# A two-layer hybrid decoder on one core: delta-rule heads in a fixed TensorE order, block diagonals filled by DMAs, S5's loads issued earlier

## The chip, the core and the metric

The kernel runs on one core of a Trainium2 chip. The core has five engines with queues of their own: PE (TensorE: matrix products), DVE (VectorE), ACT (ScalarE), POOL (GpSimd) and SP, which here only issues DMAs; POOL and ACT issue some as well. Each engine takes its queue in order, and engines wait for one another and for DMAs by semaphores. The metric is the device time of one execution, in microseconds (us).

## What is computed

x is (1024, 1024), in float32, and there are two layers. Both have the same frame: one input projection, a mixer beside a 4-head cross-attention into 256 memory tokens, one output projection over their concatenated outputs, a layer norm, an MLP with squared ReLU (1024 to 4096 to 1024) and a second layer norm.

```
def step(state, inp):                       # layer 0, per head (8 heads of 128), chunk after chunk
    v_new = ui - wi @ state                 # ui, wi: from a triangular solve inside the chunk
    attn = (qi @ ki.T) * deci
    o = (qi * exp(gci)) @ state + attn @ v_new
    state = state * exp(g_last) + (ki * exp(g_last - gci)).T @ v_new
...
st = sr + abar^t * h                        # layer 1: S5, diagonal complex scan, 64 groups of 16 channels
y  = Re(C st) + d_skip * u;  zg = gelu(y);  out = zg * sigmoid(zg @ w_glu + b_glu)
...
h = concatenate([mix, cross]) @ w_o[i]
x = layer_norm(alpha * x + h);  x = layer_norm(alpha * x + relu(x @ w1)**2 @ w2)
```

In layer 0, queries, keys and values go through a causal convolution of width 4 and SiLU, queries and keys are normalised, and the output of each head is normalised and multiplied by SiLU of a fourth projection, the gate. The triangular solve uses the inverse of (I + strictly lower part of beta k k^T times the decay) of each chunk.

## The kernel before

All big products are float32 in three fp32r products (`mm3`, L120 to L125): the weight and the activation are both split into a high and a low part. A projection of 128 columns (`proj_fm`) is 2 halves of 512 tokens times 8 steps of 128 inputs times 3, 48 products of 128x512. Its weight comes by an SP DMA into one of two raw buffers, and is split by ACT (L102) and DVE (L103) into one of two pairs of buffers.

The program is written as a sequence, and a scheduler gives each engine an order by readiness and program order. `piece()` (L73) fixes TensorE's order for what stands in it: its products go behind all those of the piece before.

Layer 0 works in tiles of 128 tokens, 8 per head, in two halves of 4:
- `gdn_a(h)` (L469) makes the keys of head h: projection, convolution, norm; the decay matrix D from prefix sums (`decay`, L457); the products `kk` (L501) and the strictly lower matrix NT, written to DRAM: its 32x32 diagonal blocks, packed by POOL into `pkd` (L508), and two masked copies (L512, L513).
- `gdn_inverse(h0)` (L516) inverts the 32x32 diagonal blocks of two heads at once, with a block in each partition: 8x8 blocks by scalar products on DVE, a round trip through DRAM (L565 to L577), then 16x16 products on POOL (L582 to L587), and the result into DRAM (L597, L598).
- `block_diag` (L600) loads such blocks packed and spreads them over a block-diagonal 128x128 tile with a DVE multiplication by a mask (L605).
- `gdn_invert_tiles` (L609) goes from 32 to 64 to 128 with five groups of four products `iv` (L623) per half, each needing the one before through DVE (`zi`, L628) or ACT.
- `gdn_b(h)` (L642) makes queries, values and gate, the inversion, and the recurrence over the 8 tiles (L698 to L726): `ks` = K S; `R` on DVE (L710); `pe` = T R (L712); `e` on ACT (L714); the outputs `po` (L716, L717); `pS` (L720); `S` on DVE (L725). Norm, transposes (`ot`, L740) and gate follow, and a DMA to `cat`.

The run takes keys three heads ahead: keys 0 and 1, the inverse of heads 0 and 1, the cross-attention with keys 2 in it, and then for each head `gdn_b(h)`, keys h+3 and, after an odd head, `gdn_inverse(h+1)`, which needs the keys of heads h+1 and h+2. In the program the inversion of a head comes behind its own queries, values and gate.

In layer 1, `s5_front` (L1293) orders pieces: U (S5's projection), Q, S, T, V (the attention's), `drive` and `read`. `s5_drive` (L1137) loads, for eight groups in two halves, G (`g1d`), two tables and H (`h1d`) by POOL DMAs, makes p1 = G u on TensorE (L1166), rotates by the tables on DVE and ACT, scans on DVE (L1175), rotates back, and lastly issues the load of the matrix M0 (`zd`). `s5_read` (L1188) makes y from M0 u and H r.

Of the kernel before, what the change touches and what calls it, by code (L numbers as in the profile page):

```python
# [28 lines left out]
class Trunk:  # L29
# [125 lines left out]
    def acc_tm(self, tau, hk, wk, add, banks=("pi", "po", "sc")):  # L155

        t0 = (tau % 4) * P
        n = len(wk)
        for c in range(2):
            ps = self.psum(banks[self.turn % 3], "tm")  # L160
            self.turn += 1
            for k in range(n):
                hi, lo = hk[k][tau // 4]
                self.mm3(ps, (hi[:, t0:t0 + P], lo[:, t0:t0 + P]), wk[k][c], k == 0, k == n - 1)
            add(c, ps)

# [102 lines left out]
    def gdn_consts(self):  # L269
# [25 lines left out]
        bd = scr[:, 3 * P:3 * P + 4]  # L295
        nc.gpsimd.memset(bd, 0.0)
        for b in range(4):
            nc.gpsimd.memset(bd[32 * b:32 * b + 32, b:b + 1], 1.0)
        self.bdm = bd
        self.early = [early[:, 2 * P + 64 * n:2 * P + 64 * (n + 1)].rearrange("p (t h) -> p t h", t=8) for n in range(2)]  # L300
        cw = scr[:, 3 * P + 8 + 13 * 64:].rearrange("p (m j) -> p m j", j=4)
# [54 lines left out]
    def gates(self, ba):  # L356
# [37 lines left out]
        gc, wd, egl, nec = self.gc, self.wd, self.egl, self.nec = G("gc"), G("wd"), G("egl"), G("nec")  # L394
# [16 lines left out]
        V.tensor_scalar(nec, nec, -1.0, None, op0=ALU.mult)  # L411
        self.beta = beta

        self.ssk, self.gam, self.ngam, self.kds, self.sk = G("ssk"), G("gam"), G("ngam"), G("kds"), G("sk")
# [16 lines left out]
    def conv_silu(self, m, xT, outs, tag, w=None):  # L431
# [17 lines left out]
        self.proj_fm(w or self.a["w_in"][m], xT, evac, "wi")  # L449
# [7 lines left out]
    def decay(self, h, hf, tag):  # L457

        nc = self.nc
        pb = self.sums(h, hf, tag)  # L460
        d = self.tile(tag, [P, 4, P], F32, "D")
        for t in range(4):
            tt = 4 * hf + t
            nc.vector.scalar_tensor_tensor(d[:, t, :], pb[:, t, :], self.gc[:, tt, h:h + 1], self.maskneg, op0=ALU.subtract, op1=ALU.min)
        nc.scalar.activation(d, d, AF.Exp)
        nc.scalar.dma_start(self.ded[h, hf], d)
        return d

    def gdn_a(self, h, xT, w=None):  # L469

        nc = self.nc
        V = nc.vector
        kT = self.kTs[h % 4]
        self.conv_silu(8 + h, xT, [kT[:, :HALF], kT[:, HALF:]], "h1", w)
        for hf in range(2):
            t4 = slice(4 * hf, 4 * hf + 4)
            pt = self.psum("pa", "kt", (P, 4, P))
            for t in range(4):
                tt = 4 * hf + t
                nc.tensor.transpose(pt[:, t, :], kT[:, tt * P:(tt + 1) * P], self.ident)  # L480
            for t in range(4):
                tt = 4 * hf + t
                nc.scalar.activation(self.jk, pt[:, t, :], AF.Square, accum_out=self.ssk[:, tt, h:h + 1])
            s = lambda x: x[:, t4, h]
            V.tensor_scalar(s(self.ssk), s(self.ssk), 4e-6, None, op0=ALU.add)
            V.reciprocal(s(self.gam), s(self.ssk))
            V.tensor_tensor(s(self.gam), s(self.gam), s(self.beta), op=ALU.mult)
            V.tensor_scalar(s(self.ngam), s(self.gam), -1.0, None, op0=ALU.mult)
            V.tensor_tensor(s(self.kds), s(self.gam), s(self.wd), op=ALU.mult)
            nc.gpsimd.tensor_tensor(s(self.sk), s(self.ssk), self.half[:, 0:4], op=ALU.pow)  # L490
            kd = self.tile("h1", [P, 4, P], F32, "kd")
            for t in range(4):
                nc.scalar.activation(kd[:, t, :], pt[:, t, :], AF.Copy, scale=self.kds[:, 4 * hf + t, h:h + 1])
            nc.sync.dma_start(self.kdd[h, hf], kd)
            d = self.decay(h, hf, "h1")
            pq = self.psum("pa", "kk", (P, 4, P))
            n = self.tile("h1", [P, 4, P], F32, "NT")
            for t in range(4):
                tt = 4 * hf + t
                c = slice(tt * P, (tt + 1) * P)  # L500
                nc.tensor.matmul(pq[:, t, :], kT[:, c], kT[:, c], start=True, stop=True)  # L501
            for t in range(4):
                tt = 4 * hf + t
                V.scalar_tensor_tensor(n[:, t, :], pq[:, t, :], self.ngam[:, tt, h:h + 1], d[:, t, :], op0=ALU.mult, op1=ALU.mult)
            pkd = self.tile("S", [P, 4, 32], F32, "pkd")
            for b in range(4):
                q = slice(32 * b, 32 * b + 32)
                nc.gpsimd.tensor_copy(pkd[q], n[q, :, q])  # L508
            nc.gpsimd.dma_start(self.ntd[h, t4].rearrange("t b j i -> (b j) t i"), pkd)
            for w, m in enumerate((self.m64, self.m128)):  # L510
                nm = self.tile("h1", [P, 4, P], F32, "nm")
                nc.gpsimd.tensor_tensor(nm, n, m.unsqueeze(1).to_broadcast([P, 4, P]), op=ALU.mult)  # L512
                nc.gpsimd.dma_start(self.ntf[h, hf, w], nm)  # L513
        return kT
# [85 lines left out]
    def block_diag(self, h, hf, w):  # L600
        nc = self.nc
        pk = self.tile("S", [P, 4, 32], F32, "pk")
        nc.sync.dma_start(pk, self.t32[w, h, 4 * hf:4 * hf + 4].rearrange("t b i c -> (b i) t c"))
        o = self.tile("h4", [P, 4, 4, 32], F32, "bd")
        nc.vector.tensor_tensor(o, pk.unsqueeze(2).to_broadcast([P, 4, 4, 32]),  # L605
                                self.bdm.unsqueeze(1).unsqueeze(3).to_broadcast([P, 4, 4, 32]), op=ALU.mult)
        return o.rearrange("p t b c -> p t (b c)")

    def gdn_invert_tiles(self, h, hf):  # L609
# [3 lines left out]
        T32, V32 = self.block_diag(h, hf, 0), self.block_diag(h, hf, 1)  # L613

        def masked(w):
            o = self.tile("h4", [P, 4, P], F32, "nm")
            nc.sync.dma_start(o, self.ntf[h, hf, w])
            return o
# [17 lines left out]
        zi = plus_i(mm4(masked(0), T32))  # L636
        T64 = keep(mm4(V32, zi), "h4")
        V64 = keep(mm4(zi, V32), "h4")
        zi2 = plus_i(mm4(masked(1), T64))
        return keep(mm4(zi2, V64), "h3")  # L640

    def gdn_b(self, h, xT, kT):  # L642
        nc = self.nc
        V = nc.vector

        qT = [self.tile("h2", [P, HALF], F32, "qT") for _ in range(2)]
        self.conv_silu(h, xT, qT, "h2")
        qe = []
        at, vs = (x.rearrange("p (t c) -> p t c", t=8) for x in self.mix[2 * (h % 2):2 * (h % 2) + 2])
        for hf in range(2):  # L650
            pt = self.psum("pa", "qt", (P, 4, P))
            for t in range(4):
                nc.tensor.transpose(pt[:, t, :], qT[hf][:, t * P:(t + 1) * P], self.ident)
            for t in range(4):
                nc.scalar.activation(self.jk, pt[:, t, :], AF.Square, accum_out=self.ssq[:, 4 * hf + t, h:h + 1])
            d = self.tile("h2", [P, 4, P], F32, "Dq")
            nc.sync.dma_start(d, self.ded[h, hf])
            pb = self.sums(h, hf, "h2")
            e = pb.rearrange("p t i -> p (t i)")
            nc.scalar.activation(e, e, AF.Exp)  # L660
            V.tensor_tensor(e, e, qT[hf], op=ALU.mult)
            qe.append(e)
            pq = self.psum("pa", "qk", (P, 4, P))
            for t in range(4):
                tt = 4 * hf + t
                nc.tensor.matmul(pq[:, t, :], kT[:, tt * P:(tt + 1) * P], qT[hf][:, t * P:(t + 1) * P], start=True, stop=True)
            for t in range(4):
                tt = 4 * hf + t
                V.scalar_tensor_tensor(at[:, tt, :], pq[:, t, :], self.gam[:, tt, h:h + 1], d[:, t, :], op0=ALU.mult, op1=ALU.mult)
        V.tensor_scalar(self.ssq[:, :, h], self.ssq[:, :, h], 5.12e-4, 5.12e-4 * 4e-6, op0=ALU.mult, op1=ALU.add)  # L670

        vT = [self.tile("h2", [P, HALF], F32, "vT") for _ in range(2)]
        self.conv_silu(16 + h, xT, vT, "h2")
        for hf in range(2):
            pt = self.psum("pa", "vt", (P, 4, P))
            for t in range(4):
                nc.tensor.transpose(pt[:, t, :], vT[hf][:, t * P:(t + 1) * P], self.ident)
# [874 lines left out]
```

## Time and profile before

| | us |
|---|---|
| median of three runs (lowest, highest) | 2930.1 (2928.14, 2931.73) |
| the profiled execution | 2924.6 |
| its span in the profile | 2922.9 |
| busy: PE, DVE, ACT, POOL | 2769.2, 1752.8, 994.0, 536.4 |
| first recurrence product of heads 0 and 5 at | 227.4, 660.5 |
| first transpose after the output projection of layer 0 at | 896.2 |

The page cuts the span into 40 slices of 73 us: layer 0's heads fill slices 0 to 11, its MLP follows, S5's front lies around 1725 to 2000, and the rest is the output projection and MLP of layer 1. A row of the order of time reads: start, length, engine, line, operation, output from inputs, shape, count, and in brackets how long the engine stood idle before it and what ended that. In a group's row the busy time comes first, the mean length in ns, then idle time.

### The profile page before, as it was taken

What the parts mean: (1) busy time and instruction counts of PE and PEld (TensorE: products, weight loads), DVE (VectorE), ACT (ScalarE), POOL (GpSimd) and SP (SyncE); (2) the same over time, 40 slices, a digit from 0 to 9 for tenths busy, and PEclk for the clock granted to TensorE, in tenths of its full rate; (3) what the DMA queues carried; (4) which work ended last, traced back from release to release, by engine and by line L of the source; (5) the groups of instructions that cost most, each with busy time, mean ns of one, the idle gap of its engine ahead of it and who ended that gap; (6) DMA issues with size and microseconds to landing.
All of it is one profiled execution on the core that took longest, in us unless ns stands there. A gap on an engine that the chain in (4) does not pass through costs nothing. (4 is left out here: it accounts for less than half of the span.)

```text
span 2922.9 us, 35948 instructions
## 1 busy us (share of the span) xinstructions
PE 2769.2 (95%) x13373; PEld 2261.3 (77%) x13373; DVE 1752.8 (60%) x3467; ACT 994.0 (34%) x2104; POOL 536.4 (18%) x785
## 2 busy tenths in 40 slices
PE   8999898888999999999999988879999999999998
PEld 6877676666788888778788877768888888888887
DVE  7766667665678687665655654464587444434446
ACT  5455344443422332232322234353222222222221
POOL 3631625535002021211110111212001000000002
PEclk9999999999999999999999999989999999999999
DMA  5433334333531132222222165555331111111111
GB/s 190 109 111 97 90 104 117 101 106 76 191 94 53 64 116 81 91 76 71 76 74 82 69 205 151 165 146 184 119 101 65 51 51 48 46 51 51 44 51 58
DMA packets 177583, 279.72 MB, mean 96 GB/s; under 512 B 86608, under 2 KB 103200, under 8 KB 177408
## 3 DMA queue, kind: packets, MB, share of 16 engines
q1 hardware_dynamic: 155776, 220.29, 23.9%
q0 software_dynamic: 19328, 52.94, 6.1%
q10 hardware_dynamic: 2304, 4.20, 0.4%
q8 instruction: 105, 1.72, 0.2%
q14 instruction: 70, 0.57, 0.1%
HBM read 209.73 MB, written 67.60 MB: 95 GB/s over the span
## 5 line engine op out<-in xcount | busy, mean ns | idle before, releaser
L260 DVE TENSOR_TENSOR y<-tm,y 128x512 f32<-128x512 f32 x448 | 308.5, 690 | 204.4 <-PE tm L125 200.5
L123 PE MATMUL w<-xTh,w1h 128*128 128x512 f32 x1024 | 400.6, 391 | 0.1
L124 PE MATMUL w<-xTl,w1h 128*128 128x512 f32 x1024 | 399.4, 390 | 0.0
L125 PE MATMUL w<-xTh,w1l 128*128 128x512 f32 x1024 | 399.0, 390 | 0.0
L123 PE MATMUL tm<-w2h,hh 128*128 128x512 f32 x1024 | 398.9, 390 | 0.0
L125 PE MATMUL tm<-w2h,hl 128*128 128x512 f32 x1024 | 398.6, 389 | 0.0
L124 PE MATMUL tm<-w2l,hh 128*128 128x512 f32 x1024 | 398.5, 389 | 0.0
L115 ACT CAST w2h<-w2r 128x512 fp32r<-128x512 f32 x128 | 76.4, 622 | 554.7 <-PE tm L125 445.8
L184 POOL TENSOR_SCALAR mv<-mv 128x1 f32<-128x1 f32 x32 | 40.5, 1266 | 1166.4 <-DVE mv L183 1166.4
L125 PEld LDWEIGHTS w<-xTh,w1l 128*128 128x128 f32 x1024 | 192.2, 188 | 40.4
L125 PEld LDWEIGHTS tm<-w2h,hl 128*128 128x128 f32 x1024 | 192.2, 188 | 39.9
L124 PEld LDWEIGHTS tm<-w2l,hh 128*128 128x128 f32 x1024 | 192.2, 188 | 39.9
L123 PEld LDWEIGHTS w<-xTh,w1h 128*128 128x128 f32 x1024 | 192.1, 188 | 39.9 <-ACT xTh L199 0.8
L123 PEld LDWEIGHTS tm<-w2h,hh 128*128 128x128 f32 x1024 | 192.2, 188 | 39.7
L124 PEld LDWEIGHTS w<-xTl,w1h 128*128 128x128 f32 x1024 | 192.3, 188 | 39.5
L213 DVE TENSOR_TENSOR hl<-w,hh 128x512 fp32r<-128x512 f32 x128 | 87.3, 688 | 167.8 <-ACT hh L212 167.8
L103 DVE TENSOR_TENSOR w1l<-w1r,w1h 128x1024 fp32r<-128x1024 f32 x62 | 75.9, 1225 | 186.1 <-ACT w1h L102 184.1
L123 PE MATMUL wi<-xTh,wih 128*128 128x512 f32 x384 | 159.1, 414 | 3.5 <-ACT zc L687 3.5
L125 PE MATMUL wi<-xTh,wil 128*128 128x512 f32 x384 | 157.6, 410 | 0.0
L124 PE MATMUL wi<-xTl,wih 128*128 128x512 f32 x384 | 157.5, 410 | 0.0
L208 ACT ACTIVATE w<-w 128x512 f32<-128x512 f32 x128 | 74.5, 582 | 167.0 <-PE w L125 161.2
L102 ACT CAST w1h<-w1r 128x1024 fp32r<-128x1024 f32 x62 | 65.4, 1054 | 185.5 <-PE w L124 154.6
(417 smaller groups left out, 5711.3 us busy)
## 6 DMA issues: line engine op xcount, KB each, us to landing
w1r<-in_w_dram SPq DMA_DIRECT2D x64, 512.0 KB, 3.4
w2r<-in_w_dram SPq DMA_DIRECT2D x64, 512.0 KB, 3.4
wir<-in_w_in_dram SPq DMA_DIRECT2D x24, 512.0 KB, 3.6
wor<-in_w_o_dram SPq DMA_DIRECT2D x24, 512.0 KB, 3.5
cat<-cat SPq DMA_DIRECT2D x24, 512.0 KB, 3.3
gb<-gcd SPq DMA_DIRECT2D x32, 256.0 KB, 4.2
ntf<-nm POOLq DMA_DIRECT2D x32, 256.0 KB, 2.9
nm<-ntf SPq DMA_DIRECT2D x32, 256.0 KB, 3.3
```

Of the source, the lines that this page charges most:

```text
L102: nc.scalar.copy(hi, r)
L103: nc.vector.tensor_tensor(lo, r, f32(hi), op=ALU.subtract)
L115: nc.scalar.copy(hi, s)
L123: nc.tensor.matmul(ps, a[0], b[0], start=start, stop=False)
L124: nc.tensor.matmul(ps, a[0], b[1], start=False, stop=False)
L125: nc.tensor.matmul(ps, a[1], b[0], start=False, stop=stop)
L184: nc.gpsimd.tensor_scalar(mv[:, 2:3], mv[:, 1:2], 1e-5, None, op0=ALU.add)
L208: nc.scalar.activation(ps, ps, AF.Relu)
L213: nc.vector.tensor_tensor(lo, ps, f32(hi), op=ALU.subtract)
L260: nc.vector.tensor_tensor(o, ps, o, op=ALU.add)
```

## The change

- `proj_steps`, `acc_steps` and `gdn_recur` are generators that yield after each small step with its length on TensorE in us. `weave` runs one step of a main generator, then steps of a fill worth `share` us, each in a piece of its own, so that TensorE's order is that of the program. `take` runs steps up to a sum.
- `gdn_recur(h)` is the main part. The fill is `gdn_fill(h+1)`: keys of head h+3, queries, values and gate of head h+1 (`gdn_projections`), with the ten inversion steps of head h+1 spread among them. The first of these steps is due 2.3 us into the fill (half of 49 / 10.5). `gdn_inverse(h+1)` is called in the projections of the odd head h, behind its queries and the keys of head h+2, so while the recurrence of head h-1 runs. The last recurrence is woven with the output projection.
- `gdn_a` becomes `gdn_keys` and `gdn_keys_out`. D is one DVE addition and four ACT exponentials with a bias; ACT multiplies D by gamma, so that NT and `at` need one DVE instruction each in place of four.
- `block_diag` fills two constant tiles, zeroed once, by four DMAs each; the packed tile and the DVE multiplication go.
- S5: G and the tables of tile m+1 are issued behind the drive of tile m, ahead of M0 and H of tile m; in odd tiles the drive comes before the scores; some PSUM banks and buffer tags differ.

The diff, cut to its core:

```diff
+    STEP = 0.68
+    def proj_steps(self, src, xT, evac, nm):
+        w = src if isinstance(src, tuple) else self.load_split(src, "w1", nm)
+        for h in range(2):
+            ps = self.psum("mm", nm)
+            for k in range(KT):
+                c = slice(k * P, (k + 1) * P)
+                self.mm3(ps, (w[0][:, c], w[1][:, c]), (xT[h][0][:, k, :], xT[h][1][:, k, :]), k == 0, k == KT - 1)
+                if k == KT - 1:
+                    evac(h, ps)
+                yield self.STEP
+    def weave(self, main, fill, share):
+        owed = 0.0
+        while True:
+            with self.piece():
+                done = next(main, self) is self
+            if done:
+                return
+            owed += share
+            while owed > 0:
+                with self.piece():
+                    took = next(fill, None)
+                if took is None:
+                    break
+                owed -= took
+    def forced(self, steps):
+        while True:
+            with self.piece():
+                took = next(steps, None)
+            if took is None:
+                return
+            yield took
+    def take(self, steps, us):
+        for took in self.forced(steps):
+            us -= took
+            if us <= 0:
+                return
...
+        nc.vector.tensor_tensor(d, pb, self.maskneg.unsqueeze(1).to_broadcast([P, 4, P]), op=ALU.add)
+        for t in range(4):
+            nc.scalar.activation(d[:, t, :], d[:, t, :], AF.Exp, bias=self.ngc[:, 4 * hf + t, h:h + 1])
+        return d
...
+        pq = self.psum("pa", "kk", (P, 4, P))
+        n = self.tile("h1", [P, 4, P], F32, "NT")
+        for t in range(4):
+            tt = 4 * hf + t
+            c = slice(tt * P, (tt + 1) * P)
+            nc.tensor.matmul(pq[:, t, :], kT[:, c], kT[:, c], start=True, stop=True)
+        V.scalar_tensor_tensor(n, pq, -1.0, d, op0=ALU.mult, op1=ALU.mult)
...
+            nc.scalar.activation(d[:, t, :], d[:, t, :], AF.Copy, scale=self.gam[:, 4 * hf + t, h:h + 1])
         nc.scalar.dma_start(self.ded[h, hf], d)
...
     def block_diag(self, h, hf, w):
-        nc = self.nc
-        pk = self.tile("S", [P, 4, 32], F32, "pk")
-        nc.sync.dma_start(pk, self.t32[w, h, 4 * hf:4 * hf + 4].rearrange("t b i c -> (b i) t c"))
-        o = self.tile("h4", [P, 4, 4, 32], F32, "bd")
-        nc.vector.tensor_tensor(o, pk.unsqueeze(2).to_broadcast([P, 4, 4, 32]),
-                                self.bdm.unsqueeze(1).unsqueeze(3).to_broadcast([P, 4, 4, 32]), op=ALU.mult)
-        return o.rearrange("p t b c -> p t (b c)")
-    def gdn_invert_tiles(self, h, hf):
+        o = self.bds[w]
+        for b in range(4):
+            q = slice(32 * b, 32 * b + 32)
+            self.nc.sync.dma_start(o[q, :, q], self.t32[w, h, 4 * hf:4 * hf + 4, b].rearrange("t i c -> i t c"))
+        return o
+    def gdn_invert_tiles(self, h):
...
+            nm = masked(hf, 0)
+            T32, V32 = self.block_diag(h, hf, 0), self.block_diag(h, hf, 1)
+            zi = plus_i(mm4(nm, T32))
+            yield 0.8
+            T64 = keep(mm4(V32, zi), "h4")
+            yield 0.8
+            V64 = keep(mm4(zi, V32), "h4")
+            nm = masked(hf, 1)
+            yield 0.8
+            zi = plus_i(mm4(nm, T64))
+            yield 0.8
+            out.append(keep(mm4(zi, V64), "h3"))
+            yield 0.8
...
+    def gdn_projections(self, h, xT):
+        half = lambda x: (next(x) for _ in range(KT))
+        more = h + 2 < 8
+        if more:
+            keys = self.gdn_keys(h + 2, xT)
+            yield from half(keys)
+            yield from half(keys)
+        self.qT[h] = [self.tile("h2", [P, HALF], F32, "qT") for _ in range(2)]
+        self.qe[h] = []
+        queries = self.conv_silu(h, xT, self.qT[h], "h2")
+        for hf in range(2):
+            yield from half(queries)
+            if more:
+                self.gdn_keys_out(h + 2, hf)
+                yield 1.2
+        if more and h % 2:
+            self.gdn_inverse(h + 1)
+        self.vT[h] = [self.tile("h2", [P, HALF], F32, "vT") for _ in range(2)]
+        values = self.conv_silu(16 + h, xT, self.vT[h], "h2")
+        for hf in range(2):
+            yield from half(values)
+            self.gdn_queries_out(h, hf)
+            yield 1.2
+        gate = self.gdn_gate(h, xT)
+        for hf in range(2):
+            yield from half(gate)
+            self.gdn_values_out(h, hf)
+            yield 0.4
+    def gdn_fill(self, h, xT, wait=0.0):
+        steps, inv = self.gdn_projections(h, xT), self.gdn_invert_tiles(h)
+        total = 49.0 if h + 2 < 8 else 35.6
+        each = (total - wait) / 10.5
+        passed = 0.0
+        due = wait + 0.5 * each
+        for took in steps:
+            yield took
+            passed += took
+            if passed >= due:
+                due += each
+                took = next(inv, None)
+                if took is not None:
+                    yield took
+        yield from inv
+    def gdn_recur(self, h):
+        nc = self.nc
+        V = nc.vector
...
+                    nc.tensor.matmul(po[:, t, :], qe[hf][:, t * P:(t + 1) * P], S, start=True, stop=False)
+                    yield
...
+    def s5_driving(self, m):
+        out = []
+        for b in range(2):
+            gs = slice(4 * b, 4 * b + 4)
+            G1 = self.s5_load("G1", "h1", self.g1d[m, :, gs])
+            out.append((G1, [self.s5_load("tab", "h2", self.tabd[x, :, 8 * m + 4 * b:8 * m + 4 * b + 4, :]) for x in range(2)]))
+        return out
+    def s5_reading(self, m):
+        M0 = self.s5t[:, 0:T] if m == 7 else self.s5t[:, T:2 * T]
+        M0 = M0.rearrange("p (g x) -> p g x", g=8)
+        z = self.zd[m]
+        self.nc.gpsimd.dma_start(M0, bass.AP(z.tensor, z.offset, [[16, 8], [8 * 240, 16], [240, 8], [1, P]]))
+        H = [self.s5_load("H1", "h2" if m == 7 else "h1", self.h1d[m, :, 4 * b:4 * b + 4, 1:9, :].rearrange("p g d o -> p g (d o)")) for b in range(2)]
+        return M0, H
...
+                if m == 0:
+                    loads[0] = self.s5_driving(0)
+                r[m] = self.s5_drive(m, loads.pop(m))
+                if m < 7:
+                    loads[m + 1] = self.s5_driving(m + 1)
...
+                drive(m)
                 S(h, 0)
                 S(h, 1)
-                drive(m)
...
-        keys = {}
-        def keys_of(h, w=None):
-            if h < 8:
-                keys[h] = self.gdn_a(h, xT, w)
-        tags = ("h4", "h3", "h2", "h2", "h2")
-        keys_of(0, w0)
-        keys_of(1)
+        self.TT, self.qT, self.qe, self.vT, self.zs, self.outs = {}, {}, {}, {}, {}, []
+        for h in range(2):
+            for _ in self.gdn_keys(h, xT, (w0, None)[h]):
+                pass
+            for hf in range(2):
+                self.gdn_keys_out(h, hf)
         self.gdn_inverse(0)
         kv = self.mem_kv(0)
-        self.memory_heads(xT, kv, tags, lambda: keys_of(2))
+        tags = ("h4", "h3", "h2", "h2", "h2")
+        fill = self.gdn_fill(0, xT, 30.0)
+        self.memory_heads(xT, kv, tags, fill)
         self.mix = self.quad(F32, "mix")
-        for h in range(8):
-            self.gdn_b(h, xT, keys.pop(h))
-            keys_of(h + 3)
-            if h % 2 and h < 7:
-                self.gdn_inverse(h + 1)
+        self.take(fill, 1e9)
+        for h in range(7):
+            fill = self.gdn_fill(h + 1, xT)
+            self.weave(self.gdn_recur(h), fill, 2.75 if h < 5 else 1.95)
+            self.take(fill, 1e9)
...
+        steps, xT, front = self.block_end(0, y)
+        self.weave(self.gdn_recur(7), steps, 2.5)
+        self.take(steps, 8.0)
+        with self.piece():
+            self.gdn_out_last()
+        for _ in steps:
+            pass
```

More of the change, by code (lines that the diff above doesn't have):

```diff
@@ L473, in gdn_a @@
         kT = self.kTs[h % 4]
[L474 to L513, printed above, removed]
@@ L643, in gdn_b, with gdn_queries_out @@
+    def gdn_queries_out(self, h, hf):
         nc = self.nc
         V = nc.vector
[L646 to L669, printed above, removed]
@@ L1281, in memory_heads @@
                 queries(h + 1, 1)
+            else:
+                self.take(last, 4.0)
             with self.piece():
```

217 lines of the change are left out of this document (133 added, 84 removed).

## The prediction

> **What bounds the kernel now.** I read the page first, then the busy time by stretch, the groups of one stretch, the waits of TensorE, and the order of time at single places.
>
> ```profile
> PE 2769.2 (95%) x13373; PEld 2261.3 (77%) x13373; DVE 1752.8 (60%) x3467; ACT 994.0 (34%) x2104; POOL 536.4 (18%) x785
> PE   8999898888999999999999988879999999999998
> ```
>
> TensorE is busy 95% of the span. The 8s lie in slices 0 to 9 (the delta-rule heads) and 24 to 26 (S5): only there can time be won. The next view gives busy time by stretch: start and end, length, then busy time and instructions of PE, PEld, DVE, ACT and POOL, the granted clock, the DMA share and GB/s.
>
> ```profile
> 171.00:896.20 725.20, 657.70 (x3503) 526.49 (x3501) 480.90 (x1025) 309.79 (x886) 233.56 (x320) 0.98 0.37 111
> 227.40:660.50 433.10, 386.11 (x2092) 307.05 (x2092) 290.68 (x650) 196.78 (x584) 179.54 (x247) 0.98 0.35 104
> 225.00:250.00 25.00, 25.00 (x154) 20.39 (x152) 13.72 (x23) 8.24 (x15) 0.00 (x0) 1.00 0.20 64
> 1725.00:2000.00 275.00, 223.26 (x1163) 191.52 (x1162) 150.60 (x297) 127.00 (x233) 55.05 (x75) 0.89 0.56 168
> ```
>
> 171 to 896.2 runs from the end of the first inverse to the first transpose of the next block: eight heads. 227.4 to 660.5 lies between the first recurrence products of heads 0 and 5, so a head takes 433.1 / 5 = 86.6 us. What TensorE must do in it follows from the groups of 171 to 896.2 and from two distances.
>
> ```profile
> L125 PE MATMUL wi<-xTh,wil 128*128 128x512 f32 x336 | 138.7, 413 | 0.0
> L124 PE MATMUL tm<-wol,chl 128*128 128x512 f32 x144 | 58.1, 403 | 0.0
> L123 PE MATMUL wz<-xTh,wzh 128*128 128x512 f32 x128 | 53.5, 418 | 5.1 <-ACT vT L442 4.9
> L623 PE MATMUL iv<-bd,zi 128*128 128x128 f32 x128 | 18.6, 291 | 0.0
> L740 PE MATMUL ot<-ident,on 128*128 128x128 f32 x64 | 10.5, 288 | 3.2 <-ACT on L734 2.3 <-DVE scr L485 0.7
> ```
> ```profile
> 230.15 0.40 PE L125 MATMUL wi<-xTh,wil 128*128 128x512 f32 x1
> 230.38 0.39 PE L123 MATMUL wi<-xTh,wih 128*128 128x512 f32 x1
> 230.86 1.16 PE L623 MATMUL iv<-zi,bd 128*128 128x128 f32 x8
> 231.78 0.48 PE L125 MATMUL wi<-xTh,wil 128*128 128x512 f32 x1
> ```
>
> Starts lie 0.23 apart for a 128x512 product (0.227 over longer stretches) and 0.92 / 8 = 0.115 for one record of a small fp32 product (two records each). Each `wi`, `tm` and `wz` row stands for three alike (1,822 products): 414 us. The small products (five `iv` groups of 128, and the recurrence, `kk` and `qk` rows of the same view) are 1,448 records or 167 us; 232 transposes take about 20. Together 601, with lost records 606 us. The gapless window 225 to 250, priced likewise, comes to 24.1 of 25.0, so 606 us run in 606 x 1.035 = 627 us at best. The stage takes 725: 98 us are loose.
>
> **Part 1, the fixed order of the heads.** TensorE's work is the same in both (11,486 and 11,472 instructions). Its order becomes the program's: a recurrence step, then 2.75 us of the next head's projections and inversion, and so on. That aims at waits like these (total us, times, longest):
>
> ```profile
> PE iv L623 <- DVE zi L628: 17.9, 9, 2.9
> PE pe L712 <- DVE R L710: 6.8, 11, 1.2
> PE ks L708 <- DVE S L725: 6.6, 12, 1.2
> ```
>
> Steps of the inversion now lie 4.7 us apart (49 / 10.5), longer than the longest wait of 2.9, so the first goes; R and S lie behind 2.75 us of cover against 1.2. But a head's fill holds 49 + 10 x 0.8 = 57 us, used up after 57 / 2.75 = 20.7 of 23 steps: about 2.5 us bare per head, 20 over eight. With some 2 for late R and S I take 22; bounds 8 (three steps) and 50 (a queue's head blocking in every head, half of today's 98).
>
> **Part 2, what the fixed order cannot step over.** The block inverse of heads 2 and 3 needs the `kk` products of head 3, and head 2's first inversion product needs its result. Before:
>
> ```profile
> 89.21 0.94 POOL L508 COPY pkd<-NT 32x128 f32<-32x128 f32 x3 [2.99 <-DVE NT L504]
> 153.79 0.82 POOL L598 DMA_DIRECT2D t<-X  x1
> 275.28 0.39 PE L501 MATMUL kk<-kT 128*128 128x128 f32 x2
> 289.49 0.61 POOL L508 COPY pkd<-NT 32x128 f32<-32x128 f32 x2 [2.35 <-PE vt L677]
> 301.28 0.40 POOL L532 COPY X<-X 128x64 f32<-128x64 f32 x2 [4.35 <-DMA X<-ntd]
> 314.35 0.55 POOL L565 DMA_DIRECT2D t<-To  x1
> 324.84 1.51 POOL L582 TENSOR_TENSOR pr<-X,st 128x512 f32<-128x512 f32 x1 [5.28 <-DMA X<-t]
> 359.50 0.83 POOL L598 DMA_DIRECT2D t<-X  x1
> 387.37 1.13 PE L623 MATMUL iv<-bd,nm 128*128 128x128 f32 x8
> ```
>
> From `pkd` to the last store takes 154.6 - 89.2 = 65.4 us for heads 0 and 1 and 360.3 - 289.5 = 70.8 for heads 2 and 3: a round trip of 11.8, scalar blocks on VectorE 13.1, another trip 10.5, products on GpSimd and stores 35.5. Today 387.4 - 275.3 = 112 us lie between `kk` and `iv`, so nothing waits: all of head 1's work and head 2's queries, values and gate may run between.
>
> After, the first inversion step of head 2 is due 2.3 us into head 2's fill, ahead of nearly all of that. The changed order has, between the last `kk` of head 3 and the first `iv` of head 2, 108 products of 128x512 (values, gate, and 12 of the next keys): 24.5 us; five inversion steps 4.8; four and a half recurrence steps 5.3; four `qk` 1.9; transposes 1.7. Sum 38.2, at best 40 us. Heads 5 to 4 and 7 to 6 repeat it. The chain after:
> - `kk` to `pkd`: 14.2 in these rows. The decay already carries gamma, and one VectorE product makes NT, but in VectorE's queue it stands behind a `zi` whose matmul comes 15 products later (4 us). I take 7; bounds 4 and 14.2.
> - `pkd` to the last store, unchanged code: 68, between the two; bounds 65.4 and 73 (70.8 and some 2 above it).
> - last store to `iv`: landing, four issues on SP, landing.
>
> ```profile
> t<-To POOLq DMA_DIRECT2D x8, 128.0 KB, 2.6
> pk<-t SPq DMA_DIRECT2D x32, 64.0 KB, 3.4
> ```
>
>   2.6 + 1 for the issues + 3.4 = 7; bounds 5 and 10.
>
> 82 us against 40 of cover: TensorE stands 42 us, three times, 126 in all. Bounds 34 (4 + 65.4 + 5 = 74.4) and 57 each. Nothing passes it, since TensorE takes its queue in order. On SP the stored blocks' loads also stand ahead of weight loads, but the next two weights are already in: nothing. Heads 0 and 1 keep 111 us of work between (cross-attention): no stall.
>
> After a stall the clock is low. S5's longest gap shows it:
>
> ```profile
> 1957.00:1962.00 5.00, 3.91 (x18) 3.94 (x19) 5.00 (x11) 2.46 (x5) 0.76 (x1) 0.50 0.26 72
> 1960.36 0.41 PE L125 MATMUL sc<-kv,ql 128*128 128x256 f32 x1
> 1960.58 0.41 PE L123 MATMUL sc<-kv,qh 128*128 128x256 f32 x1
> ```
>
> Granted 0.50, and 0.22 us per 128x256 product, half of a 128x512's 0.227 being 0.114. Some 4 us at half speed cost 2 each, 6 in all.
>
> GpSimd's products may come faster in a stall. In this trace the first product instruction (L582) takes 1.51 us at 324.84, with VectorE three fifths busy.
>
> The Trainium skill, "SBUF — State Buffer", section "SBUF: two separate sides", says that VectorE with two SBUF inputs and a GpSimd instruction that reads SBUF hold one port pair in turn, the other blocking. In a stall VectorE has little to do; by that rule an estimate of 4 us off each inverse makes the sum 12 us lower. The row cannot tell, and I leave it out of the sum.
>
> **Part 3, small pieces.** The block diagonal loses this multiplication and gets its blocks by four DMAs each.
>
> ```profile
> L605 DVE TENSOR_TENSOR bd<-pk,scr x32: 673/683/2687, 190.7 to 792.4; 128x512 f32<-128x512 f32 x32
> ```
>
> 32 x 0.683 = 22 us of VectorE go, and 96 issues on SP come; VectorE is 60% busy and SP mostly waits, so nothing on the path, beyond the 1 us counted. Without VectorE's slack the gain would be 22 at most. Four ACT exponentials in place of one, and four scalings, cost ACT (34% busy) some 16 x 2 us, beside TensorE; their late end is in the bound 14.2. Weaving the last recurrence with the output projection is in the 606.
>
> Stage: 627 + 126 + 6 + 22 = 781, against 725: +56.
>
> **Part 4, S5's loads.**
>
> ```profile
> 1742.19 1.22 PE L1166 MATMUL p<-s5t,G 128*128 128x128 f32 x4 [5.44 <-DMA G<-g1d]
> 1809.12 1.22 PE L1166 MATMUL p<-s5t,G 128*128 128x128 f32 x4 [8.30 <-DMA G<-g1d]
> 1877.23 1.01 PE L1166 MATMUL p<-s5t,G 128*128 128x128 f32 x3 [10.40 <-DMA G<-g1d]
> 1958.09 2.05 PE L1166 MATMUL p<-s5t,G 128*128 128x128 f32 x8 [10.47 <-DMA G<-g1d]
> ```
> ```profile
> G<-g1d POOLq DMA_DIRECT2D x16, 256.0 KB, 10.0
> s5t<-zd POOLq DMA_DIRECT2D x8, 512.0 KB, 10.7
> ```
>
> TensorE waits 34.6 us for G, which queues on POOL behind the previous read's matrix (10.7 to landing). G and the tables are now issued a drive earlier: those waits go, with 3 us of cold clock. What is late next is the read: its matrix and H now stand behind six loads, and the even tiles' read comes only two projection halves later (48 products, 11 us of work). I put 2 us on each of four: -38 + 8 = -30. Bounds -40 and -5.
>
> **Sum.** +56 - 30 = +26 on the profiled execution's 2924.6: 2950.6. It ran 5.5 us under the median of the runs, 2930.1; so 2956.
>
> **Rivals.**
> - Faster: the stalls are short and the weave tight. With 34 each, 8 of weave and S5 at -38: 627 + 102 + 6 + 8 = 743, +18 - 38 = -20: 2910. For it: the first inverse took 65.4, and products may run faster beside an idle VectorE. Against: the second inverse took 70.8. With 22 and -30 held, the stall decides at (725 + 30 - 627 - 6 - 22) / 3 = 33 us, that is, a chain of 73.
> - S5 wins nothing: the reads wait for H and the matrix as long as drives did for G; -5 in place of -30: 2981. For it: the queue moves the same bytes. Against: loads then have a whole tile's work ahead of them.
> - Much slower: `kk` to `pkd` stays 14.2, the inverse 73, so 55 per stall (165), and weave 40, since a late instruction at the head of VectorE's or ACT's queue now holds TensorE: 627 + 165 + 6 + 40 = 838, +113 - 30: 3013.
> - The order is fixed on paper only, and TensorE steps over the stall: the stage as before, S5 -30: 2900. The changed order speaks against it.
>
> **Numbers.** Forecast 0.52, S5 without gain 0.12, much slower 0.12, short stalls 0.20, stepped over 0.04. A measurement of this kernel tells 0.2%, about 6 us, from no change. The forecast's own range is 2935 to 2978; the range over the cases runs from the short stalls to the upper half of the bounds: 2908 to 2998. Faster takes the last two cases, same 0.07 of the forecast's lower end, slower the rest.
>
> **What would show it.** Three idle stretches of TensorE of 34 to 57 us, at the start of heads 2, 4 and 6, each ended by a DMA into `bd`, with GpSimd's products in them; `iv` waiting on `zi` below 5 us in total elsewhere; no wait for G over 2 us in S5, and short ones on H or the matrix. I am wrong if these stalls are under 33 us, if weave waits exceed 50, or if S5 keeps its gaps.

## The result, and the profile after

| | us |
|---|---|
| before, median of four runs | 2930.9 |
| after, median of four runs (lowest, highest) | 3011.2 (3009.9, 3014.5) |
| ratio after to before | 1.0274 (95% interval 1.0256 to 1.0292) |
| span of the profiled execution, before and after | 2922.9, 3008.2 |

The change makes the kernel 80 us slower; 26 was forecast, and the top of the forecast's widest range was 2998. In the page after, TensorE's row of 40 slices has its low digits where the delta-rule heads are:

```profile
PE 2775.3 (92%) x13373; PEld 2298.0 (76%) x13373; DVE 1697.4 (56%) x3284; ACT 1015.5 (34%) x2214; POOL 511.6 (17%) x782
PE   7998688586899999999999998888999999999998
```

Slices 4 to 9 fell from 8s and 9s to 6s, 8s and one 5; TensorE's work did not grow. By stretch:

```profile
171.00:994.40 823.40, 668.23 (x3554) 569.90 (x3552) 436.92 (x886) 334.87 (x992) 211.22 (x321) 0.89 0.33 98
```

The first transpose of the next block comes at 994.4 in place of 896.2: the stage takes 823.4, not 725.2, so 98 us are lost there. From that place to the end the profiled execution takes 3008.2 - 994.4 = 2013.8 against 2922.9 - 896.2 = 2026.7: S5 gains 13. The granted clock of the stage (column before the last two) is 0.89 in place of 0.98. TensorE's waits in the stage (total, times, longest):

```profile
PE iv L666 <- DMA bd<-t: 69.3, 3, 23.9
PE ks L818 <- DVE S L835: 58.3, 16, 5.0
PE po L836 <- ACT e L826: 11.5, 6, 2.4
```

All waits of the stage come to 155 us; before they were 66. The first row is the stall that the prediction named. Its chain for heads 2 and 3, in order of time from POOL's, SP's and TensorE's rows:

```profile
272.57 1.06 PE L554 MATMUL kk<-kT 128*128 128x128 f32 x8
280.46 1.27 POOL L559 COPY pkd<-NT 32x128 f32<-32x128 f32 x4 [2.90 <-DVE scr L845]
345.40 0.83 POOL L648 DMA_DIRECT2D t<-X  x1
348.14 1.74 SPq L655 DMA_DIRECT2D bd<-t  x4
351.53 2.05 PE L666 MATMUL iv<-bd,nm 128*128 128x128 f32 x8 [23.94 <-DMA bd<-t]
```

From `kk` to `iv` 351.5 - 272.6 = 79 us: 7.9 to `pkd`, 65.8 to the end of the last store, 5.3 to `iv`. The second row of waits was not forecast in that size. One case, from ACT's, DVE's and TensorE's rows:

```profile
261.59 0.40 ACT L547 ACTIVATE D<-D,scr 128x128 f32<-128x128 f32 x1 [1.05 <-DVE scr L539]
261.90 1.12 ACT L544 ACTIVATE kd<-kt,scr 128x128 f32<-128x128 f32 x4
262.90 0.99 ACT L547 ACTIVATE D<-D,scr 128x128 f32<-128x128 f32 x3
263.99 0.69 DVE L555 SCALAR_TENSOR_TENSOR NT<-kk,D 128x512 f32<-128x512 f32 x1 [2.23 <-ACT D L547]
264.60 0.34 DVE L835 SCALAR_TENSOR_TENSOR S<-S,scr,pS 128x128 f32<-128x128 f32 x1
264.98 0.58 PE L818 MATMUL ks<-S,kT 128*128 128x128 f32 x1 [4.67 <-DVE S L835]
```

`pS` was computed at 257.4. Its update S, 0.34 us of work, runs at 264.6: ahead of it in VectorE's queue stand the convolution of the queries, the sums for gamma, and NT, which waits for ACT. TensorE, whose order is now fixed, stands 4.67 us, although the projections behind `ks` in its queue need no S. After such a stall TensorE is slow, as behind the long one:

```profile
355.08 0.63 PE L125 MATMUL wi<-xTh,wil 128*128 128x512 f32 x1
355.51 0.63 PE L123 MATMUL wi<-xTh,wih 128*128 128x512 f32 x1
...
356.97 0.39 PE L124 MATMUL wi<-xTl,wih 128*128 128x512 f32 x1
357.19 0.39 PE L125 MATMUL wi<-xTh,wil 128*128 128x512 f32 x1
```

0.43 from start to start, then 0.22. The granted clock was 0.52 from 351.5 to 356.9, and 1.00 from 254 to 264, ahead of the product that waited until 265. In the stage 113 products of 128x512 start 0.34 to 0.55 before the next such product; what they take over 0.23 adds up to 22 us (before: 30 products, 6 us).

In S5, the waits for G are gone; these are there now:

```profile
PE pT L947 <- ACT p L933: 23.6, 3, 7.9
PE py L1325 <- DVE r L1313: 9.0, 3, 4.8
```

The transposes of the softmax wait 7.9 us in each of three odd tiles.

### The profile page after: what moved, and what is told of

It is laid out like the page before. It is cut to its first block, busy times and chain, and to the rows that moved or that the text cites. A ratio compares the mean times of both kernels' runs of the same rounds, so it can differ in the third digit from the quotient of the medians.

```text
span 3008.2 us, 35949 instructions
## 1 busy us (share of the span) xinstructions
PE 2775.3 (92%) x13373; PEld 2298.0 (76%) x13373; DVE 1697.4 (56%) x3284; ACT 1015.5 (34%) x2214; POOL 511.6 (17%) x782
## 4 chain that ended last, share of the span: by engine, by line
PE 73%; DVE 8%; DMA 5%; POOL 5%; ACT 4%; issue 3%; SPq 1%; POOLq 0%; DVEq 0%; ACTq 0%
PE tm L125 9%; PE tm L124 9%; PE tm L123 9%; PE w L125 7%; PE w L124 7%; PE w L123 7%; PE wi L123 2%; PE wi L124 2%; PE wi L125 2%; PE iv L666 2%; POOL pr L636 1%; DMA gb<-gcd 1%; POOL pr L632 1%; PE wg L123 1%; PE wg L124 1%
## 5 line engine op out<-in xcount | busy, mean ns | idle before, releaser
L123 PE MATMUL wi<-xTh,wih 128*128 128x512 f32 x384 | 172.3, 449 | 0.0
```

The costliest lines, as they stand in the source:

```text
L123: nc.tensor.matmul(ps, a[0], b[0], start=start, stop=False)
```

## The experiments

Three theories were at stake: the chain that the fixed order cannot step over (69 us), the heads of other engines' queues (58 us), and in S5 the drive ahead of the scores (24 us). Times are medians; the ratio is to the kernel before, measured beside it.

**e1: the inversion later.**

```diff
-            fill = self.gdn_fill(h + 1, xT)
+            fill = self.gdn_fill(h + 1, xT, 22.0 if h % 2 else 0.0)
```

> The changed kernel, but the inversion steps of heads 2, 4 and 6 are due only from 22 us into their fill, in place of 0. Theory (a chain that TensorE's fixed order cannot step over): the chain from the kk products to the loads of bd stays near 80 us, the cover grows by some 25 us, so the three waits of iv for bd (69.3 us) go to under 6 in all, with 2 us of low clock each: 70 to 76 us faster than the changed kernel, near 2938. The waits of ks for S (58 us) stay. Rival (the inversion as such is the bound, its steps squeezed into 27 us): iv then waits for zi, or pe for the last iv, and at least half of the 69 us comes back.

Measured: 2988.5, ratio 1.0191 (1.0169 to 1.0213), 23 us faster than the changed kernel. Neither theory nor rival: no `iv` waits for bd or zi for long, but `pS` waits 19.7 and 19.4 us for e, in place of the stalls of heads 2 and 4. The first of the two, from SP's, DVE's and TensorE's rows:

```profile
329.02 0.91 SPq L807 DMA_DIRECT2D kdl<-kdd  x2
357.66 0.32 SPq L655 DMA_DIRECT2D bd<-t  x1
367.30 0.69 DVE L512 TENSOR_TENSOR D<-gb,scr 128x512 f32<-128x512 f32 x1 [15.12 <-DMA gb<-gcd]
373.09 0.79 PE L830 MATMUL pS<-e,kdl 128*128 128x128 f32 x2 [19.67 <-ACT e L826]
```

SP issues nothing from 329.9 to 357.7: the load of bd stands at its head, waiting for the inverse. Behind it stands the load of the prefix sums (gb) of the next keys; DVE waits for it with D, ACT behind that with D's exponentials, and e behind those. The stall had moved from TensorE's queue to SP's. In the fill of head 6 there are no next keys, and no such wait.

**e6: e1, with the loads of bd from GpSimd's queue.**

```diff
-            self.nc.sync.dma_start(o[q, :, q], self.t32[w, h, 4 * hf:4 * hf + 4, b].rearrange("t i c -> i t c"))
+            self.nc.gpsimd.dma_start(o[q, :, q], self.t32[w, h, 4 * hf:4 * hf + 4, b].rearrange("t i c -> i t c"))
```

> The kernel e1 (inversion steps of heads 2, 4, 6 due from 22 us of fill), with the loads of bd issued from GpSimd's queue, where they stand behind the stores of the inverse anyway, in place of SP's. Theory (in e1 the bd loads, waiting at the head of SP's queue for the inverse, held the prefix sums of the next keys behind them, then D on VectorE and ACT, then e): the three waits of 19 us of pS are gone, no wait for bd over 5 us is left; 65 to 80 us faster than the changed kernel, near 2938. Rival (the wait only moves on, to the next thing in GpSimd's queue or to TensorE's iv): less than 40 us faster, and some wait of 10 us or more, three times.

Measured: 2941.9, ratio 1.0021 (1.0011 to 1.0032), 69 us faster than the changed kernel, as the theory had it (of the waits of 19 us that it names, e1 has two, not three). There is no wait for bd among the long ones:

```profile
PE ks L818 <- DVE S L835: 42.8, 12, 5.9
PE pS L830 <- ACT e L826: 21.6, 4, 7.5
```

**e9: the queue alone**, the same edit without the later inversion.

> The changed kernel, but the loads of bd are issued from GpSimd's queue, and the inversion is due as in the changed kernel. Theory (TensorE stands for the chain, and SP's queue was only the second thing in line): the three waits of iv for bd stay at 20 to 26 us each, and the time is within 12 us of the changed kernel. Rival (the gain of e6 came from the queue, not from the later inversion): over 40 us faster.

Measured: 3008.1, ratio 1.0263 (1.025 to 1.0276), 3 us faster, which cannot be told from no change. The queue alone gains nothing, the later inversion alone 23 us, both together 69:

```profile
PE iv L666 <- DMA bd<-t: 72.8, 3, 24.6
```

**e2: gamma back on DVE.**

```diff
-        for t in range(4):
-            nc.scalar.activation(d[:, t, :], d[:, t, :], AF.Copy, scale=self.gam[:, 4 * hf + t, h:h + 1])
         nc.scalar.dma_start(self.ded[h, hf], d)
...
-        V.scalar_tensor_tensor(n, pq, -1.0, d, op0=ALU.mult, op1=ALU.mult)
+        for t in range(4):
+            V.scalar_tensor_tensor(n[:, t, :], pq[:, t, :], self.ngam[:, 4 * hf + t, h:h + 1], d[:, t, :], op0=ALU.mult, op1=ALU.mult)
```

(and likewise, with gam, for the query tile)

> The changed kernel, but gamma is again multiplied in by DVE (four products each for NT and for the query tile, as in the kernel before) in place of ACT's scaling of D. Theory (NT, waiting for ACT's scaling at the head of DVE's queue, holds the update of S behind it, and TensorE with it): the waits of ks for S fall from 58.3 to under 15. Those that lie between kk of the odd head and iv of the even head (some 9 us for each of three) only move into the wait for bd, which grows to 28 or 30 us each; the rest with its low clock is gained: 30 to 45 us faster than the changed kernel. Rival (S is late because DVE and ACT as a whole have too much to do in a recurrence step): the waits stay above 40 us, and more DVE instructions make it no faster.

Measured: 2999.4, ratio 1.0223 (1.0198 to 1.0248), 12 us faster. The waits for S went only from 58 to 45, as the rival had it, so NT's wait for ACT was the smaller part; but the rival had no gain at all, and 12 us are one. The waits, and DVE's rows at the same place as above:

```profile
PE iv L668 <- DMA bd<-t: 52.1, 3, 25.8
PE ks L821 <- DVE S L838: 45.4, 15, 4.3
PE pS L833 <- DMA kdl<-kdd: 23.4, 2, 21.2
```
```profile
253.47 0.75 DVE L496 SCALAR_TENSOR_TENSOR qT<-cv,scr,qT 128x512 f32<-128x512 f32 x1
254.14 0.68 DVE L673 TENSOR_TENSOR zi<-iv,ident 128x512 f32<-128x512 f32 x1
...
256.46 1.13 DVE L557 SCALAR_TENSOR_TENSOR NT<-kk,scr,D 128x128 f32<-128x128 f32 x4
257.50 0.34 DVE L838 SCALAR_TENSOR_TENSOR S<-S,scr,pS 128x128 f32<-128x128 f32 x1
```

VectorE is simply busy with the fill: a half of the queries, an inversion step and a half of the keys end together, and S comes last. (In head 6 the load of kdl stands behind the first load of bd on SP, so its stall carries another name.)

**e5: the burst taken apart.** The second part of the keys' work goes into the middle of a half of the queries.

```diff
         d = self.decay(h, hf, "h1")
+        yield
         pt = self.psum("pa", "kt", (P, 4, P))
...
-            yield from half(queries)
-            if more:
-                self.gdn_keys_out(h + 2, hf)
-                yield 1.2
+            if more:
+                out = self.gdn_keys_out(h + 2, hf)
+                next(out)
+            for k, took in enumerate(half(queries)):
+                yield took
+                if more and k == 3:
+                    for _ in out:
+                        pass
+                    yield 1.2
```

> The changed kernel, but the second part of the keys' work (kt, sums, gamma, kk, NT) is issued in the middle of a half of the queries in place of right behind its end, so that it no longer falls on VectorE together with the convolution of that half; kk comes 2.7 us of fill earlier. Theory (the update of S waits behind a burst of the fill's work in VectorE's queue, whatever NT itself waits for): the waits of ks for S fall from 58 to under 30, those for bd grow or shrink by no more than 5 each; 20 to 40 us faster than the changed kernel, near 2980. Rival (VectorE and ACT are simply too slow for a recurrence step in 2.75 us of fill): the waits stay above 45 us, under 10 us faster.

Measured: 2992.6, ratio 1.0198 (1.018 to 1.0217), 19 us faster, between the two:

```profile
PE iv L667 <- DMA bd<-t: 55.6, 3, 19.9
PE pS L836 <- ACT e L832: 30.7, 11, 3.9
PE ks L824 <- DVE S L841: 11.8, 3, 4.9
```

The waits for S fell to 12 us, so the burst made them. But 31 us of waits for e appeared: the sums, kd and D of the keys now stand ahead of e in ACT's queue (in one case `pe` starts at 254.7 and e at 260.9).

**e3 and e4: S5's order.** In e3 the scores come before the drive again, in e4 both projection halves before the transposes.

```diff
e3:
-                drive(m)
                 S(h, 0)
                 S(h, 1)
+                drive(m)
e4:
                 U(m + 2, 0)
-                T(h, 0)
                 U(m + 2, 1)
+                T(h, 0)
                 T(h, 1)
```

> The changed kernel, but in S5's odd tiles the scores come before the drive again, with the loads still issued a drive earlier. Theory (the new waits of pT for the softmax, 23.6 us in three, come from the drive no longer standing between scores and transposes, while the waits for G went because of the earlier issue): pT waits under 9, G waits still under 2 us each: 12 to 20 us faster than the changed kernel. Rival (the order was what took the waits for G away): G waits of over 4 us come back, and the time is within 6 us of the changed kernel.

Measured: 2987.2, ratio 1.0189 (1.0167 to 1.0211), 24 us faster and more than the 12 to 20 of the theory; one wait for G of 0.5 us, and of the transposes' waits 4.8 us in three are left. From the first transpose of the block behind the heads (996.6) to the end (2985.8) it takes 1989.2, 37 us less than the kernel before.

> The changed kernel, but in S5's odd tiles both projection halves come before the first transposes of the softmax. Theory: 24 more products of 128x512 (5.5 us) stand behind the scores, so each of the three waits of pT falls from 7.9 to 2.4: 16 us faster than the changed kernel, with up to 3 more for low clock. Rival (ACT and DVE do the softmax only after work of the projection, which now comes earlier too): the waits fall by less than half, under 9 us faster.

Measured: 3005.7, ratio 1.0247 (1.0223 to 1.0272), 5 us faster: the rival's number, hardly more than no change, and not by its mechanism. The softmax stands where it stood (16.5 us from the first score to the first transpose in both kernels), and the first transposes wait 2.5 in place of 7.9, as the theory had it. But the projection half that now goes ahead had stood between the first transposes and the second, which need the results of the first to be read out (`pTl`); they now stand right behind those and wait up to 2.6 us:

```profile
PE pT L947 <- ACT p L933: 8.1, 6, 2.5
PE pT L947 <- DVE pTl L951: 7.3, 3, 2.6
```

**e7 and e10: one part alone on the kernel before.** e7 has S5's part of the diff, with the scores before the drive; e10 has `block_diag` and its constant tiles.

> The kernel before, with only S5's loads issued a drive earlier (and the changed banks and tags), and the scores before the drive as in the kernel before. Theory (this part of the change is a gain by itself, as the prediction's 30 us, given back in part by the order): 32 to 40 us faster than the kernel before, near 2894, with no wait for G over 2 us. Rival (what S5 gains hangs on the state in which the heads leave the queues): under 20 us faster.

Measured: 2894.5, ratio 0.9865 (0.9848 to 0.9881), 40 us faster than the kernel before. One wait for G of 1.7 us is left. In its trace 37 us are gained behind the heads (1989.4 against 2026.7); the heads end at 902.9, in place of 896.2.

> The kernel before, with only the block diagonals filled by four DMAs each in place of one DMA and the DVE product. Theory (off the path, as the prediction has it): within 6 us of the kernel before. Rival (96 more issues on SP, or two tiles in place of a rotating tag, hold the inversion up): over 8 us slower, with iv waiting for bd.

Measured: 2933.3, ratio 1.0012 (1.0003 to 1.0021): 2 us slower by the medians, 1 to 6 by the interval. iv waits 4.5 us for bd, once. But TensorE stands once for longer, from SP's and its own rows:

```profile
PE iv L620 <- DMA bd<-t: 4.5, 1, 4.5
354.95 3.17 SPq L603 DMA_DIRECT2D bd<-t  x7
363.90 0.79 PE L705 MATMUL ks<-S,kT 128*128 128x128 f32 x2 [16.77 <-DVE S L722]
```

From 340 to 354.9 SP issues nothing: the loads of bd stand at its head until the inverse is stored (354.0). Behind them stands a load of prefix sums (358.7) for which ACT waits, then VectorE, and S behind that: the wait of e1, in the scheduler's order. The first transpose of the next block still comes only 2 us later (898.3), so the whole is nearly even, but not because nothing waits. Whether the DMAs or the order that the scheduler chose beside them put the wait there is open.

**e8, e11 and e12: the parts together.** e8 is the changed kernel with e3, e5 and e6, and the inversion due from 30 us (24 in head 6). e11 adds e2's edit; e12 instead sets the share to 2.48.

```diff
-            fill = self.gdn_fill(h + 1, xT)
+            fill = self.gdn_fill(h + 1, xT, (30.0 if h < 5 else 24.0) if h % 2 else 0.0)
-            self.weave(self.gdn_recur(h), fill, 2.75 if h < 5 else 1.95)
+            self.weave(self.gdn_recur(h), fill, 2.48 if h < 5 else 1.95)      (e12 alone)
```

> The changed kernel with e3, e5 and e6 together, and the inversion steps due from 30 us of fill (24 for head 6). Theory (the fixed order itself costs nothing; three queues' heads and one order do): the gains add up, some 70 + 30 + 24 us less the part of the S waits that lay in the cover: 2875 to 2905, faster than the kernel before and about level with e7. Rival (the fixed order loses to the scheduler's own order even so, since TensorE cannot step over any wait): above 2915.

Measured: 2902.3, ratio 0.9889 (0.9874 to 0.9904), inside the theory's range, near its upper end, and 8 us behind e7: so far the fixed order still costs something. What is left:

```profile
PE pe L830 <- DVE R L826: 22.9, 7, 7.9
PE pS L836 <- ACT e L832: 19.2, 8, 3.9
PE po L842 <- ACT e L832: 13.3, 6, 2.4
PE ks L824 <- DVE S L841: 12.6, 4, 5.2
```

> The kernel e8, with gamma multiplied in by DVE again. Theory (in e8 what is left of the waits in the weave, e on ACT 19 us and R on DVE 23 us, comes from ACT's queue holding four scalings, four copies and the sums ahead of e): the waits of pS for e fall below 10, those of pe for R stay or grow by up to 5: 5 to 15 us faster than e8. Rival (moving work from ACT to DVE only moves the wait): within 5 us of e8, with R or S later by what e is earlier.

Measured: 2877.8, ratio 0.9817 (0.9801 to 0.9832), the fastest of all: 24 us faster than e8 by the medians, 21 by the ratios (each beside its own runs of the kernel before), more than the theory had.

```profile
PE pe L833 <- DVE R L829: 18.5, 9, 6.0
PE pS L839 <- ACT e L835: 14.6, 6, 2.9
PE po L845 <- ACT e L835: 13.3, 6, 2.4
PE ks L827 <- DVE S L844: 7.3, 4, 3.0
```

The waits for e did not fall below 10; three of the four rows fell a little, 14 us in sum. The first recurrence product comes 5 us earlier as well (228.9 in place of 233.9). That taking the scalings off ACT gains this is shown; through which of the waits most of it goes is not.

> The kernel e8, with 2.48 us of fill behind each recurrence step in place of 2.75, so that the 57 us of fill last for all 23 steps of heads 0 to 4. Theory (the prediction's bare steps at the end of a head): the waits of po for e at the head's end fall from 13 to under 6, five times 2.4 us with 1 to 2 of low clock: 8 to 18 us faster than e8. Rival (less cover in every step costs more): the waits for S, R and e in the middle of the heads grow by as much or more, not over 3 us faster.

Measured: 2905.3, ratio 0.9911 (0.9895 to 0.9926), 3 us slower than e8, which cannot be told from no change: the rival's time. The waits of po fell from 13.3 to 5.0, as the theory had it. In the middle of the heads S waits 8.8 us longer and R 14.6 shorter, so S, R and e together did not grow, against what the rival had. New are 7 us of waits for kdl, and `iv` waits some 10 us more, for several things. Cover is only shifted.

```profile
PE ks L824 <- DVE S L841: 21.4, 6, 4.6
PE pS L836 <- ACT e L832: 17.1, 9, 4.3
...
PE pe L830 <- DVE R L826: 8.3, 3, 3.4
PE pS L836 <- DMA kdl<-kdd: 7.2, 3, 3.1
...
PE po L842 <- ACT e L832: 5.0, 4, 1.7
```

## Why the prediction was wrong, point by point

| term | forecast | measured |
|---|---|---|
| chain from `kk` to `iv` | 82 | 79 |
| three waits for bd | 126 | 69 |
| other waits of the weave | 22 | 155 - 69 = 86 |
| low clock | 6 | 22 |
| the rest of the stage | 627 | 823 - 155 - 22 = 646 |
| stage | 781 | 823 |
| S5 | -30 | -13 |
| sum against before | +26 | +85 (spans) |

- **The direction and the chain were right, the size of the stall was not.** The chain has the length forecast, it stands where it was forecast, and e1, e6 and e9 show together that TensorE stands for it. The wait itself is only 23 us, not 42, because the 38 us of products meant to cover it took 55: the waits for S (3.65, 1.54 and 3.76 us between 280 and 318), their low clock and the waits for e lie in the cover. A wait in there costs nothing further, one elsewhere does. So this term came out 57 us too high and the others of the stage 99 too low; with the stall as measured and all else as forecast, the sum would have been 31 us faster than before, so the right direction is in part luck. Two of the prediction's own signs of being wrong came: stalls under 33 us, and waits of the weave above 50.
- **The step that failed most is in part 1: "R and S lie behind 2.75 us of cover against 1.2".** 1.2 us is what S took when the scheduler let TensorE go on; in the fixed order, S takes its place in VectorE's queue behind whatever of the fill ended just before, up to 7 us (257.4 to 264.6). The count of waits, 22 with a bound of 50, should have gone by each queue: what stands ahead of S, R and e at the step where a half of a projection ends. The steps at the ends of the heads, to which the 22 went, measured 11.5. The rival "much slower" came to nearly the time measured, 3013, which is luck: its late instruction at the head of a queue did hold TensorE, but waits of the weave came to 86, not 40, and its other half, 14.2 and 73 in the chain and stalls of 55, did not happen.
- **Low clock** was counted for three stalls. Each of the waits of 3.6 to 5 us brings it as well, so 6 became 22; the kernel before already had 6.
- **The rest, 627,** was taken from one gapless window of 25 us. By the same count as in the table the kernel before has 725 - 66 - 6 = 653: its loose 98 us were 72 of waits and low clock, and the rest stayed where it was (646).
- **Part 3, "Four ACT exponentials ... and four scalings ... beside TensorE", was costed at nothing.** Undoing the scalings gives 12 us in e2 and 24 on top of e8: ACT was only 34% busy, but these stood ahead of NT and e. That the block diagonals by DMAs cost nothing on the whole was right to some 2 us (e10), in spite of one wait of 16.8 us.
- **Part 2's "On SP ... nothing" was right for the changed kernel only.** It looked at the weight loads behind the blocks, not at the prefix sums. As soon as the stall leaves TensorE, SP's queue is the next in line (e1), and it was once in the scheduler's order too (e10).
- **Part 4** had the loads right: G's waits went, and e7 gives 40 us by the medians, the upper bound, and 37 behind the heads by the traces. It left out the step that the diff moves, the drive ahead of the scores in odd tiles: 24 us (e3). The price forecast for late reads, 8 us, did not come: no product waits for M0 or H. That `py` waits 9 us is another thing, r from VectorE, and its nearness to 8 is luck.
- The rule of the Trainium skill on the port pair ("SBUF — State Buffer", "SBUF: two separate sides") was weighed and left out of the sum. An inverse has eight groups of products on GpSimd. In both kernels the first instruction of the first four groups takes mostly 1.5 us and that of the last four mostly 1.25 to 1.3, with VectorE busy or idle, so only like groups can be compared. (In the prediction's row at 324.84 VectorE was busy 0.28 of 1.60 us, not three fifths.) The last four, before and in the stall:

```profile
342.10:357.20 15.10, 10.27 (x50) 6.84 (x48) 8.93 (x22) 4.84 (x14) 13.49 (x21) 0.95 0.14 52
329.40:342.80 13.40, 0.00 (x0) 0.00 (x0) 2.02 (x4) 1.14 (x4) 11.82 (x20) 0.63 0.00 0
```

  With VectorE busy 8.9 us they took 15.1, with VectorE busy 2.0 us 13.4. The trace agrees in direction: 1.7 us an inverse, not the 4 of that estimate. That the port pair is the reason is not shown.

## What to carry to other kernels

Fixing one engine's order makes every other queue's head a bound: price each wait of the fixed engine by what stands ahead of its releaser in that releaser's own queue, DMA queues included, and not by the wait seen while a scheduler could still step around it. Find the longest chain that leaves the engine and comes back, and put its use at least that much of the engine's work later; then look which queue holds the waiting instruction, since the stall moves there. In a change of several parts, try each alone: here one part gained 40 us, one nothing, and the fixed order, with the small pieces that stayed beside it, gained over S5's part alone (ratio 0.9865) only once its inversion, its queues and its bursts were moved and gamma was back on VectorE (0.9817; without the last 0.9889). The heads then end at 890.4, in place of 896.2 before and 902.9 in e7.

## What the runs showed that was not expected

- Waits of 3.6 to 5 us are enough for the low clock: thirteen waits for S of this length stand in the heads of the changed kernel, and behind each of them 3 to 9 products of 128x512 lie 0.43 us apart in place of 0.23, for 1 to 4 us. There is no sharp bound in these traces: a wait of 2.4 us (at 436.2) left no slow product, one of 2.5 in the kernel before (at 310.2) left three. The Trainium skill, "TensorE: Matmul & The Clock Gate", section "What's actually happening", gives about 3.4 us for an idle window and as much for the warm-up; the waits for S and the stretches behind them are of this order, the 2.5 us wait is shorter.
- A wait for a DMA at the head of SP's queue cost 20 us of TensorE twice (e1) and 17 once (e10), through the next prefix sums and the instructions of VectorE and ACT behind them, none of which needs the inverse.
